# Normalizing retention on VectorE one tile at a time, one bank for four score products, and a buffer of its own for half of the last down-projection weights

## The chip, the cores and the metric

The kernel runs on one core of a Trainium2 chip. The engines are TensorE (PE: matmul, with its weight loads shown as PEld), VectorE (DVE), ScalarE (ACT), GpSimd (POOL) and SyncE (SP, which here only issues transfers). The metric is the time of one execution on the device in microseconds; lower is better. Before the change the median of three runs is 1147.84 us (1147.78 to 1148.55).

## The reference, cut to what matters

One layer of a diffusion backbone works on 640 tokens of 1024 channels: 128 context tokens and 512 latent tokens. After a modulated RMSNorm two token mixers run side by side, a bidirectional retention and a grouped-query attention; both are gated and summed, and a gated MLP of width 2816 with a three-tap convolution follows. All numbers are fp32.

Two places matter here. The first is retention, which runs in chunks of 128 tokens with 8 heads (64 channels of q and k, 128 of v), and its norm per head:

```
scores = einsum("bhnid,bhnjd->bhnij", qc, kc) * intra_decay
intra  = einsum("bhnij,bhnjv->bhniv", scores, vc)
cross  = einsum("bhnid,nbhdv->bhniv", qc * q_decay, s_prev)
o      = rms_scale(o_f + o_b)              # per token and head, over 128 channels
yr     = silu(rg) * o
```

The second is the end: `x = x + g2 * ((silu(g) * a) @ w_down)`, and one last RMSNorm over the 1024 channels of each token.

## The kernel before, in words

**Tiles.** The 640 tokens are five tiles of 128 tokens. Fp32 products are made from a high and a low part (fp32r), so that one product is three matmuls (`mm3`, lines 157 to 159; in transposed form lines 195 to 197, and 1579 to 1582 in the MLP). A weight block of 1024 or 2048 columns is loaded into one of two `weights.raw` buffers (line 134, issued by SP). ScalarE then copies its high part into a `weights.wh` tile, of which there are eight (line 145), and the low part is made either by VectorE (line 150) or by a negated ScalarE copy and an accumulating transfer that POOL issues (lines 147 and 148). In the MLP's units the same is done by lines 1556 to 1564.

**Retention.** Two groups of four heads times five tiles make ten steps. They pass through three functions in a pipeline. `ret_a` (lines 920 to 942) transposes q on TensorE into a PSUM bank (927), copies it out twice on ScalarE (932) and once with the decay on VectorE (936), transposes k into a second bank (939), and copies that on ScalarE (941). `ret_b`, one step later, makes the four score products of the heads (949) and multiplies them by the decay matrix on VectorE (952). `ret_c`, one step later still, makes the outputs (960 and 962), squares and copies them on ScalarE (965 and 966) and sums the squares on VectorE (967). Behind the last tile of each group, `ret_d` works out the inverse root of the five tiles (14 small VectorE instructions, lines 208 to 220) and scales the five tiles (973). PSUM tiles named `aux` have three banks: a step needs one for q, one for k, two for the scores and one for the output.

Beside the ten steps runs `rg0`, the gate projection for the first four heads, whose matmuls fill TensorE between the steps; one part of it is drawn behind every third yield of `retention`. Its evacuation (lines 1001 to 1004) takes tanh on ScalarE and then two VectorE instructions, the second of which multiplies the gate into the same `f0.s` tiles that line 973 scales. The projection for the other four heads follows.

**Order.** In this stage a planner sets the order on each engine ahead of time, from the order in the program and from costs of its own, and it also chooses which free PSUM bank a tile gets. On the chip every engine then works strictly through its own list. In the MLP the order of TensorE is written out by hand (`seq`), and those of the other engines are left to the planner.

**The end.** The MLP makes the 2816 channels in pairs of 128. `w_down` is applied in groups of four channel blocks; the last group (`last_group`, lines 1655 to 1670) is split in two column halves (g = 0 and 1), and each loads 2048 weight columns into one `weights.raw` buffer. Of these the first 1024 are prepared early (`prep(0)`) and used for tiles 0 to 3 while the last convolutions and gates (lines 1366 to 1382) are still being made; the second 1024 (`prep(1)`) follow. Then `last` runs: the rest of the matmuls, the gated residual add on VectorE (1454 and 1459), the squares on ScalarE (1476), and the final norm and the stores. The load for g = 1 comes in `pump`, which calls a group's `load` as soon as fewer than two loaded groups still have weights to prepare.

Of the kernel before, what the change touches and what calls it, by code (L numbers as in the profile page):

```python
# [18 lines left out]
P = 128  # L19
# [51 lines left out]
def hybrid_step(ctx: ExitStack, tc: tile.TileContext, a: dict, o: dict):  # L71
    nc = tc.nc
# [18 lines left out]
    V = nc.vector  # L91
# [11 lines left out]
    for i, n in enumerate(("c", "c_ctx", "norm1_g", "norm2_g")):  # L103
        src = a[n].rearrange("(k p) -> k p", p=P) if n == "c_ctx" else a[n].rearrange("o (k p) -> (o k) p", p=P)
# [24 lines left out]
    def load_w(src, kk, n, lo_eng=None):  # L129
        return w_split(w_raw(src, kk, n), kk, n, lo_eng)  # L130

    def w_raw(src, kk, n):
        raw = wp([P, 4 * 512], F32, tag="raw", bufs=2)
        nc.sync.dma_start(raw[:, :kk * n].rearrange("p (k n) -> p k n", n=n), src.rearrange("(k p) n -> p k n", p=P))
        return raw

    def w_split(raw, kk, n, lo_eng=None):
        hs, ls = [], []
        step = 1024 // n
        for k0 in range(0, kk, step):  # L140
            w = min(step, kk - k0) * n
            rv = raw[:, k0 * n:k0 * n + w]
            hi = wp([P, 1024], F32R, tag="wh", bufs=8)[:, :w]
            lo = wp([P, 1024], F32R, tag="wh", bufs=8)[:, :w]
            nc.scalar.copy(hi, rv)  # L145
            if lo_eng == "dma":
                nc.scalar.activation(lo, rv, AF.Copy, scale=-1.0)
                nc.gpsimd.dma_start(lo, rv, accum_op=ALU.add)
            else:
                (lo_eng or V).tensor_sub(lo, rv, hi.bitcast(F32))  # L150
            for k in range(w // n):
                hs.append(hi[:, k * n:(k + 1) * n])
                ls.append(lo[:, k * n:(k + 1) * n])
        return hs, ls
# [6 lines left out]
    def run(gen):  # L161
        for _ in gen:
            pass
# [39 lines left out]
    def rsqrt(pool, ss, n, inv_n, post=1.0):  # L203
        m = pool([P, n], tag=f"nm{n}", bufs=2)
        it = pool([P, n], I32, tag=f"ni{n}", bufs=2)
        y = pool([P, n], tag=f"ny{n}", bufs=2)
        tt = pool([P, n], tag=f"nt{n}", bufs=2)
        V.tensor_scalar(m, ss, inv_n, EPS, op0=ALU.mult, op1=ALU.add)
        V.tensor_scalar(it, m.bitcast(I32), 1, None, op0=ALU.logical_shift_right)
        V.tensor_scalar(y.bitcast(I32), it, -1, 0x5F3759DF, op0=ALU.mult, op1=ALU.add)  # L210
        V.tensor_scalar(m, m, -0.5, None, op0=ALU.mult)
        for _ in range(3):
            if n == 1:
                V.scalar_tensor_tensor(tt, y, m, y, op0=ALU.mult, op1=ALU.mult)
            else:
                V.tensor_mul(tt, y, y)
                V.tensor_mul(tt, tt, m)
            V.scalar_tensor_tensor(y, tt, 1.5, y, op0=ALU.add, op1=ALU.mult)  # L218
        if post != 1.0:
            V.tensor_scalar(y, y, post, None, op0=ALU.mult)  # L220
        return y
# [84 lines left out]
    aux = Pool("aux1", 3, space=PSUM)  # L306
# [273 lines left out]
    for i in (1, 0):  # L580
        ct, st = ctab[i], stab[i]
# [70 lines left out]
    aux = Pool("aux2", 2, space=PSUM)  # L652
# [132 lines left out]
    aux = Pool("aux3", 3, space=PSUM)  # L785
# [20 lines left out]
    for c in range(KD):  # L806
        if c % 2 == 0:
            w = load_w(a["w_att_o"][0, :, c * P:(c + 2) * P], 8, 256)
# [14 lines left out]
    def r2k():  # L823
        return rp([P, 512], tag="r2k", bufs=7)
# [3 lines left out]
    dmat = rp([P, 8, P])  # L828
# [87 lines left out]
    st = states()  # L916
# [26 lines left out]

    def ret_b(t, hh, qt, kt):
        at_ = r2k().rearrange("p (h i) -> p h i", h=4)
        psc = [aux([P, 512], tag="aux") for _ in range(2)]
        for j in range(2):
            for par in range(2):
                nc.tensor.matmul(psc[par][:, j * P:(j + 1) * P], kt[:, j * P:(j + 1) * P], qt[:, j, par, :],
                                 start=True, stop=True)  # L950
        for par in range(2):
            V.tensor_mul(at_[:, par::2, :], psc[par][:, :256].rearrange("p (h i) -> p h i", h=2),
                         dmat[:, 4 * hh + par:4 * hh + 4:2, :])
        return at_

    def ret_c(t, hh, qd, at_):
# [12 lines left out]
    def ret_d(hh):  # L969
        rso = rsqrt(rs2, sso[:, hh].rearrange("p t h -> p (t h)"), 4 * NT, 1.0 / P, post=0.5)  # L970
        for t in range(NT):
            ov = rvv[hh][:, :, t, :]
            nc.gpsimd.tensor_mul(ov, ov, rso[:, 4 * t:4 * t + 4].unsqueeze(2).to_broadcast([P, 4, P]))  # L973

    def conv_load(after):
        nc.gpsimd.tensor_copy(cw[:, :, 0], after)
        for i in range(3):
            nc.sync.dma_start(cw[:, i, :], a["conv_w"][0, i].rearrange("(c p) -> p c", p=P))
        nc.sync.dma_start(cw[:, 3, :], a["conv_b"][0].rearrange("(c p) -> p c", p=P))

    def retention():
        gr = [(t, hh) for hh in range(2) for t in range(NT)]
        sa, sb = {}, {}
        for i in range(len(gr) + 2):
            if i < len(gr):
                sa[i] = ret_a(*gr[i])
            if i == 1:
                conv_load(sa[0][2][:, :4])
            if 0 <= i - 1 < len(gr):
                sb[i - 1] = ret_b(*gr[i - 1], sa[i - 1][0], sa[i - 1][2])  # L990
            yield
            if 0 <= i - 2 < len(gr):
                ret_c(*gr[i - 2], sa[i - 2][1], sb[i - 2])
                if i - 2 in (4, 9):
                    ret_d(gr[i - 2][1])
            yield

    def evac_rg(g):
        def f(t, ps):
            th = r2k()  # L1000
            nc.scalar.activation(th, ps, AF.Tanh, scale=0.5)
            V.scalar_tensor_tensor(th, th, 1.0, ps, op0=ALU.add, op1=ALU.mult)
            ov = rvv[g][:, :, t, :]
            V.tensor_mul(ov, ov, th.rearrange("p (h d) -> p h d", h=4))
        return f
# [6 lines left out]
    for i, _ in enumerate(retention()):  # L1012
        if i % 3 == 2:
            next(rg0, None)
# [242 lines left out]
    w_up, w_down = a["w_up"][0], a["w_down"][0]  # L1257
# [21 lines left out]
    def h2_trans(t):  # L1279
        c = int(t == 0)  # L1280
        c0 = t * P
        for g in range(2):
# [6 lines left out]
            for j in range(4):  # L1289
# [5 lines left out]
                else:  # L1295
# [5 lines left out]
                   first=(lambda: [x + y for x, y in zip(*wo0[1:3])], lambda: wo0[3]))  # L1301
    run(wo_a)
    wo = [w_split(wo1[1], 4, 512), load_w(w_out[512:, 512:], 4, 512)]
    raw = w_raw(w_up[:, :256], 8, 256)
# [32 lines left out]
    t7 = Pool("t7", side="right")  # L1337
# [306 lines left out]
    fs = list(range(NF - 4, NF))  # L1644
# [10 lines left out]
    def last_group(g):  # L1655
        st = {}

        def load():
            st["raw"] = w_raw(w_down[fs[0] * P:, g * 512:(g + 1) * 512], 4, 512)

        def prep(h):
            def go():
                w = w_split(st["raw"][:, 1024 * h:1024 * (h + 1)], 2, 512, "dma" if h else None)
                ws[g] = [x + y for x, y in zip(ws.get(g, ([], [])), w)]
            return go

        items = [lambda t=t: last_mm(t, g * 512, 512, (0, 1)) for t in (0, 2, 1, 3)]
        return load, [(prep(0), 2, items)], items, prep(1)
# [118 lines left out]
```

## Time and profile before

| what | before |
|---|---|
| median of three runs | 1147.84 us |
| the profiled execution's own time | 1147.93 us |
| its span, first to last instruction | 1146.1 us |
| TensorE busy | 1116.3 us (97%) |
| weight loads of TensorE busy | 1006.6 us (88%) |
| VectorE busy | 841.5 us (73%) |
| ScalarE busy | 598.8 us (52%) |
| POOL busy | 154.4 us (13%) |
| granted clock of TensorE | 0.998 |

All times below are microseconds from the start of the span. The page gives busy time by engine, the waits say which instruction waited for which, and the timeline lists instructions in order of time with start, duration, engine, line, output and inputs, and, in square brackets, the idle time of the engine before it and what ended it. A TensorE row's duration reaches over the start of the next row, since matmuls are pipelined: the distance from one start to the next is what one matmul costs.

### The profile page before, as it was taken

The page shows a single profiled execution, that of the slowest core. Times are in us where ns is not written, and L with a number is a line of the kernel's source. Part 1 is how long each engine was busy: PE and PEld are TensorE (multiplying, and loading weights), DVE is VectorE, ACT ScalarE, POOL GpSimd, SP SyncE. Part 2 cuts the span into 40 slices and gives each one's busy share as a digit, 9 for nine tenths or more (in the row PEclk, how much of TensorE's full clock was granted, in tenths as well). Part 3 has the DMA queues.
Part 4 walks back from the last instruction along what each step waited for, and adds up shares of the span by engine and source line. Part 5 has one row for each costly group of instructions (what it writes and reads, how often), then busy time and mean ns, then how long its engine had stood idle before and what let it go on. Part 6 is the DMA issues. An engine that isn't in the chain of part 4 may idle for free.

```text
span 1146.1 us, 17450 instructions
## 1 busy us (share of the span) xinstructions
PE 1116.3 (97%) x6725; PEld 1006.6 (88%) x6725; DVE 841.5 (73%) x1464; ACT 598.8 (52%) x1127; POOL 154.4 (13%) x181
## 2 busy tenths in 40 slices
PE   5999999999999999999999999999999999999996
PEld 4788899999978878878999989999899899899985
DVE  4566977759969946565847648968687598589878
ACT  5355756553243334543346436678557476575463
POOL 0042200000000010021003132012111111121012
PEclk9999999999999999999999999999999999999999
DMA  9742111007846343311218937456657646666462
GB/s 308 242 150 74 38 37 38 26 13 230 305 141 218 130 138 48 39 38 37 74 37 174 286 134 220 128 117 121 142 142 159 155 76 165 136 122 167 119 129 110
DMA packets 132611, 147.92 MB, mean 129 GB/s; under 512 B 27160, under 2 KB 101992, under 8 KB 132272
## 3 DMA queue, kind: packets, MB, share of 16 engines
q1 hardware_dynamic: 103152, 115.59, 31.4%
q0 software_dynamic: 29104, 31.10, 17.2%
q8 instruction: 53, 0.87, 0.3%
q14 instruction: 30, 0.25, 0.1%
q10 hardware_dynamic: 272, 0.11, 0.0%
HBM read 115.05 MB, written 8.67 MB: 108 GB/s over the span
## 4 chain that ended last, share of the span: by engine, by line
PE 83%; DVE 8%; ACT 5%; issue 2%; DMA 1%; ACTq 0%; DVEq 0%; POOL 0%
DMA weights.raw.414_10656<-in_w_down 1%; DVE x1.u1.1_6299 L1459 1%; DMA weights.raw.247_7695<-in_w_down 0%; DMA const.u2.2_72<-in_b_mod 0%; DVE x1.u1.1_6299 L1508 0%; DVE x1.u1.1_6299 L1471 0%; DVE weights.raw.395_10305 L1556 0%; DVE x1.u1.1_6299 L1266 0%; DVE x1.u1.1_6299 L1466 0%; PE mm3.mm.72_6140 L1139 0%; DVE acts.u2.2_91 L430 0%; PE mm1.mm.11_294 L159 0%; PE mm7.mm.8_7506 L1582 0%; PE mm7.mm.41_9512 L1581 0%; PE mm7.mm.38_9263 L1582 0%
## 5 line engine op out<-in xcount | busy, mean ns | idle before, releaser
L814 POOL DMA_DIRECT2D spill.u2.2_2891<-f1.s.1_1160 x1 | 0.6, 594 | 129.7 <-DVE mod.u3.3_2846 L602 129.7
L1111 POOL DMA_DIRECT2D weights.wh.164_5834<-weights.raw.156_5767 x1 | 1.3, 1327 | 86.6 <-DVE f1.s.9_5178 L1150 86.6
L1596 DVE TENSOR_TENSOR t7.u4.4_6787<-t7.u4.4_6787,const.u1.1_70 128x320 f32<-128x320 f32 x10 | 4.9, 493 | 10.1 <-ACT const.u1.1_70 L1595 10.1
L910 DVE SCALAR_TENSOR_TENSOR ret2.u1.1_4174<-ret2.u1.1_4174,const.u11.11_86 64x128 f32<-64x128 f32 x24 | 6.8, 339 | 6.4 <-ACT ret2.u1.1_4174 L903 6.3
L973 POOL TENSOR_TENSOR f0.s.5_3419<-f0.s.5_3419,ret2.ny20.13_4765 128x512 f32<-128x512 f32 x5 | 5.5, 1124 | 38.4 <-DVE ret2.ny20.13_4765 L220 38.4
L912 DVE SCALAR_TENSOR_TENSOR ret2.u1.1_4174<-ret2.u1.1_4174,const.u11.11_86 64x128 f32<-64x128 f32 x24 | 6.6, 381 | 4.7 <-ACT ret2.u1.1_4174 L905 4.7
L150 DVE TENSOR_TENSOR weights.wh.113_4364<-weights.raw.111_4361,weights.wh.112_4363 128x1024 fp32r<-128x1024 f32 x1 | 1.2, 1224 | 11.4 <-ACT weights.wh.112_4363 L145 11.4
L427 ACT CAST acts.u1.1_90<-f0.s.2_104 128x640 fp32r<-128x640 f32 x4 | 2.9, 728 | 9.5 <-DVE f0.s.2_104 L425 9.5
L973 POOL TENSOR_TENSOR f0.s.6_3420<-f0.s.6_3420,ret2.ny20.20_4981 128x512 f32<-128x512 f32 x5 | 5.0, 1040 | 19.7 <-DVE ret2.ny20.20_4981 L220 19.7
L297 POOL DMA_DIRECT2D mod.acc.24_3626<-in_b_mod x2 | 1.7, 861 | 43.5 <-ACT weights.wh.94_3862 L145 43.5
L582 POOL TENSOR_TENSOR p1.u1.1_604<-p1.u3.3_608,p1q.u1.1_598 128x512 f32<-128x512 f32 x1 | 1.3, 1313 | 44.3 <-DMA p1.u4.4_610<-in_cache_k 44.3
L551 ACT ACTIVATE f0.s.3_710<-f0.s.3_710,p1q.ny20.11_878 128x128 f32<-128x128 f32 x20 | 6.0, 388 | 2.5 <-DVE p1q.ny20.11_878 L218 2.5
L444 PE MATMUL aux1.aux.1_134<-const.u1.1_70,const.u2.2_72 80*128 80x80 f32 x1 | 0.4, 367 | 6.9 <-DMA const.u2.2_72<-in_b_mod 6.9
L427 ACT CAST acts.u1.1_90<-f0.s.1_103 128x640 fp32r<-128x640 f32 x4 | 2.9, 726 | 8.0 <-DVE f0.s.1_103 L425 7.9
L145 ACT CAST weights.wh.67_3284<-weights.raw.66_3282 128x1024 fp32r<-128x1024 f32 x1 | 1.1, 1050 | 11.3 <-PE mm3.mm.8_3125 L196 11.3
L145 ACT CAST weights.wh.77_3516<-weights.raw.76_3514 128x1024 fp32r<-128x1024 f32 x1 | 1.1, 1055 | 11.2 <-PE mm3.mm.16_3382 L196 11.2
L1113 DVE TENSOR_TENSOR weights.wh.152_5686<-weights.raw.151_5632,weights.wh.152_5686 128x512 fp32r<-128x512 f32 x1 | 0.7, 697 | 8.3 <-ACT weights.wh.152_5686 L1104 8.3
L1470 DVE TENSOR_TENSOR x1.u1.1_6299<-x1.u1.1_6299,gate.u1.1_6285 128x512 f32<-128x512 f32 x10 | 6.7, 684 | 0.0
L1503 POOL TENSOR_TENSOR x1.u1.1_6299<-x1.u1.1_6299,weights.raw.422_10856 128x512 f32<-128x512 f32 x3 | 4.9, 1632 | 12.6 <-ACT x1.tm.111_10869 L1476 9.8
L145 ACT CAST weights.wh.92_3858<-weights.raw.91_3856 128x1024 fp32r<-128x1024 f32 x1 | 1.1, 1057 | 10.5 <-PE mm3.mm.26_3653 L158 10.5
L551 ACT ACTIVATE p1.u4.4_610<-p1.u4.4_610,p1.ny10.15_660 128x128 f32<-128x128 f32 x10 | 3.0, 388 | 6.5 <-DVE p1.ny10.15_660 L218 6.5
L150 DVE TENSOR_TENSOR weights.wh.83_3657<-weights.raw.81_3654,weights.wh.82_3656 128x1024 fp32r<-128x1024 f32 x1 | 1.2, 1224 | 7.0 <-ACT weights.wh.82_3656 L145 7.0
(6899 smaller groups left out, 4935.1 us busy)
## 6 DMA issues: line engine op xcount, KB each, us to landing
spill.u1.1_2890<-x1.u1.1_6299 POOLq DMA_DIRECT2D x5, 512.0 KB, 3.6
xin.u1.1_102<-in_x_sample SPq DMA_DIRECT2D x4, 512.0 KB, 4.7
p0.u5.5_119<-in_w_mod SPq DMA_DIRECT2D x2, 1024.0 KB, 9.9
p0.u6.6_125<-in_w_mod SPq DMA_DIRECT2D x2, 1024.0 KB, 14.6
p0.u7.7_128<-in_w_mod SPq DMA_DIRECT2D x2, 1024.0 KB, 12.8
gate.u1.1_6285<-spill.u3.3_2892 SPq DMA_DIRECT2D x2, 1024.0 KB, 4.2
x1.u1.1_6299<-in_x_sample SPq DMA_DIRECT2D x4, 512.0 KB, 10.4
out_y_sample<-x1.u1.1_6299 SPq DMA_DIRECT2D x8, 256.0 KB, 2.0
```

The source lines that it names most:

```text
L145: nc.scalar.copy(hi, rv)
L150: (lo_eng or V).tensor_sub(lo, rv, hi.bitcast(F32))
L297: nc.gpsimd.dma_start(accs[v][0:1, c, :], a["b_mod"][0:1, col:col + DM], accum_op=ALU.add)
L427: nc.scalar.copy(hT[0][:, k, :], xk)
L551: nc.scalar.activation(x[:, j], x[:, j], AF.Copy, scale=rstd[:, j:j + 1])
L910: V.scalar_tensor_tensor(Ss[0:64, hh, st + 1, j], Ss[0:64, hh, st, j], cdsel[0:64, h:h + 1], Ss[0:64, hh, st + 1, j], op0=ALU.mult, op1=AL ...
L912: V.scalar_tensor_tensor(Ss[64:128, hh, 2 - st, j], Ss[64:128, hh, 3 - st, j], cdsel[64:128, h:h + 1], Ss[64:128, hh, 2 - st, j], op0=ALU. ...
L973: nc.gpsimd.tensor_mul(ov, ov, rso[:, 4 * t:4 * t + 4].unsqueeze(2).to_broadcast([P, 4, P]))
L1459: V.tensor_add(x1[:, t, gs], x1[:, t, gs], down_mul(ps, t, c0))
L1470: V.tensor_mul(x1[:, t, gs], x1[:, t, gs], gb[:, t == 0, gs])
L1503: eng.tensor_mul(x, x, fg[:, c0:c0 + 512])
L1596: V.tensor_sub(his[1], his[1], u3[i])
```

## The change

There are three parts. In `ret_b` the four score products go to the four quarters of one PSUM bank, where they went to two halves of two banks, and one VectorE instruction of 512 columns multiplies them by the decay, where two of 256 did. In `ret_d` the scaling goes from GpSimd to VectorE, and one tile is scaled per step of the following pipeline instead of five together; for the second group the five follow at the end of `retention`. In `last_group` the first half of the weights for g = 1 gets a buffer of its own (`rawl`, in pool `t7`) and a transfer of its own; the second half goes to a `weights.raw` buffer, by another transfer.

```diff
 def ret_b(t, hh, qt, kt):
-        psc = [aux([P, 512], tag="aux") for _ in range(2)]
+        psc = aux([P, 512], tag="aux")
         for j in range(2):
             for par in range(2):
-                nc.tensor.matmul(psc[par][:, j * P:(j + 1) * P], kt[:, j * P:(j + 1) * P], qt[:, j, par, :],
+                h = 2 * j + par
+                nc.tensor.matmul(psc[:, h * P:(h + 1) * P], kt[:, j * P:(j + 1) * P], qt[:, j, par, :],
                                  start=True, stop=True)
-        for par in range(2):
-            V.tensor_mul(at_[:, par::2, :], psc[par][:, :256].rearrange("p (h i) -> p h i", h=2),
-                         dmat[:, 4 * hh + par:4 * hh + 4:2, :])
+        V.tensor_mul(at_, psc.rearrange("p (h i) -> p h i", h=4), dmat[:, 4 * hh:4 * hh + 4, :])
...
 def ret_d(hh):
         for t in range(NT):
+            yield
             ov = rvv[hh][:, :, t, :]
-            nc.gpsimd.tensor_mul(ov, ov, rso[:, 4 * t:4 * t + 4].unsqueeze(2).to_broadcast([P, 4, P]))
+            V.tensor_mul(ov, ov, rso[:, 4 * t:4 * t + 4].unsqueeze(2).to_broadcast([P, 4, P]))
...
 def retention():
+        norm = iter(())
         for i in range(len(gr) + 2):
...
             yield
+            next(norm, None)
             if 0 <= i - 2 < len(gr):
                 ret_c(*gr[i - 2], sa[i - 2][1], sb[i - 2])
                 if i - 2 in (4, 9):
-                    ret_d(gr[i - 2][1])
+                    norm = ret_d(gr[i - 2][1])
+                    next(norm)
             yield
+        run(norm)
...
 def last_group(g):
         def load():
-            st["raw"] = w_raw(w_down[fs[0] * P:, g * 512:(g + 1) * 512], 4, 512)
+            src = w_down[fs[0] * P:, g * 512:(g + 1) * 512]
+            if g == 0:
+                raw = w_raw(src, 4, 512)
+                st["raw"] = [raw[:, 1024 * h:1024 * (h + 1)] for h in range(2)]
+                return
+            first = t7([P, 1024], tag="rawl")
+            nc.sync.dma_start(first.rearrange("p (k n) -> p k n", n=512), src[:2 * P].rearrange("(k p) n -> p k n", p=P))
+            st["raw"] = [first, w_raw(src[2 * P:], 2, 512)]

         def prep(h):
             def go():
-                w = w_split(st["raw"][:, 1024 * h:1024 * (h + 1)], 2, 512, "dma" if h else None)
+                w = w_split(st["raw"][h], 2, 512, "dma" if h else None)
```

## Prediction

> **What bounds the kernel.** I read the page first, then busy time in stretches, then TensorE's waits, and the timelines where these point.
>
> ```profile
> span 1146.1 us, 17450 instructions
> PE 1116.3 (97%) x6725; PEld 1006.6 (88%) x6725; DVE 841.5 (73%) x1464; ACT 598.8 (52%) x1127; POOL 154.4 (13%) x181
> ```
>
> TensorE is the bound nearly everywhere, so an edit is worth the time in which TensorE stands, plus what it moves in the tail behind the last matmul. Stretches around the two edited places (columns: stretch, then PE, PEld, DVE, ACT, POOL busy):
>
> ```profile
> 490.00:500.00 10.00, 7.76 (x48) 6.22 (x47) 7.26 (x8) 5.35 (x11) 4.82 (x5) 1.00 0.05 13
> 500.00:510.00 10.00, 9.90 (x79) 8.79 (x78) 6.15 (x11) 4.47 (x10) 0.00 (x0) 1.00 0.27 94
> 1100.00:1110.00 10.00, 9.40 (x57) 8.47 (x56) 4.33 (x9) 3.58 (x5) 0.01 (x1) 1.00 0.36 107
> 1110.00:1120.00 10.00, 9.01 (x40) 6.93 (x38) 7.28 (x10) 6.30 (x9) 1.72 (x2) 1.00 0.74 157
> 1120.00:1130.00 10.00, 9.86 (x42) 7.71 (x43) 9.16 (x13) 3.62 (x10) 3.49 (x3) 1.00 0.01 2
> ```
>
> TensorE's waits, the longest here:
>
> ```profile
> PE aux3.aux.57_4861 L960 <- DVE ret.r2k.67_4845 L936: 2.2, 1, 2.2
> ```
>
> **Part 1, scaling on VectorE.** The 2.2 us hole, on VectorE, POOL and TensorE:
>
> ```profile
> 490.48 0.39 PE L157 MATMUL mm3.mm.41_4360<-weights.wh.119_4640,acts.u1.1_90 128*128 128x512 f32 x1
> 490.71 0.39 PE L158 MATMUL mm3.mm.41_4360<-weights.wh.120_4641,acts.u1.1_90 128*128 128x512 f32 x1
> ...
> 492.41 1.51 DVE L1004 TENSOR_TENSOR f0.s.5_3419<-f0.s.5_3419,ret.r2k.64_4823 128x512 f32<-128x512 f32 x1 [1.58 <-POOL f0.s.5_3419 L973]
> 493.85 2.06 DVE L150 TENSOR_TENSOR weights.wh.128_5080<-weights.raw.126_5077,weights.wh.127_5079 128x1024 fp32r<-128x1024 f32 x1
> 495.82 0.68 DVE L936 TENSOR_TENSOR ret.r2k.67_4845<-aux3.aux.53_4836,ret.u3.3_3418 128x512 f32<-128x512 f32 x1
> 497.09 1.21 DVE L150 TENSOR_TENSOR weights.wh.130_5084<-weights.raw.126_5077,weights.wh.129_5083 128x1024 fp32r<-128x1024 f32 x1
> 501.05 0.69 DVE L1004 TENSOR_TENSOR f0.s.5_3419<-f0.s.5_3419,ret.r2k.70_4886 128x512 f32<-128x512 f32 x1
> 489.34 5.48 POOL L973 TENSOR_TENSOR f0.s.5_3419<-f0.s.5_3419,ret2.ny20.13_4765 128x512 f32<-128x512 f32 x5 [38.44 <-DVE ret2.ny20.13_4765 L220]
> 493.92 0.40 PE L158 MATMUL mm3.mm.42_5002<-weights.wh.123_5010,acts.u1.1_90 128*128 128x512 f32 x1
> 496.56 0.49 PE L960 MATMUL aux3.aux.57_4861<-f0.s.6_3420,ret.r2k.63_4802 128*128 128x128 f32 x2 [2.24 <-DVE ret.r2k.67_4845 L936]
> ```
>
> The gate product (L1004) waits 1.58 us for POOL's scaling of its tile; then it and the weight subtraction (L150) run beside POOL at 1.51 and 2.06 us, where without POOL the same shapes take 0.69 and 1.21. Behind them stands the q product (L936), which frees the bank that the output matmul (L960) needs. The delay is 1.58 + 0.82 + 0.85 = 3.25 us on VectorE; on TensorE, 496.56 − 493.92 less one 512-column step (490.48 to 490.71, 0.23) is 2.4 us.
>
> The change takes POOL out: producer and consumer stand on one engine in program order, nothing runs beside them, and the 2.4 us go. In exchange VectorE gets ten 128x512 products at 0.69 (the L1004 row has the same shape and operands' places). The first five: 3.45 us into five steps. VectorE is busy 7.26 + 6.15 = 13.4 of the 20 us there, of which 1.67 is the slowing; with them it is about 15.2, and it waits for ScalarE's square before its sum (L967), which is the gap that hides them:
>
> ```profile
> 505.89 0.69 DVE L967 TENSOR_REDUCE const.u13.13_88<-ret.r2k.74_4924 128x4 f32<-128x512 f32 x1 [2.05 <-ACT ret.r2k.74_4924 L965]
> 514.17 0.18 DVE L220 TENSOR_SCALAR ret2.ny20.20_4981<-ret2.ny20.20_4981 128x20 f32<-128x20 f32 x1
> 519.75 1.23 DVE L150 TENSOR_TENSOR weights.wh.133_5189<-weights.raw.131_5186,weights.wh.132_5188 128x1024 fp32r<-128x1024 f32 x1 [5.40 <-ACT weights.wh.132_5188 L145]
> ```
>
> The other five follow at 514.35 and end at 517.8, inside the 5.40 us in which VectorE is idle. Without that cover each costs 0.69, 6.9 in all. Term: **−2.4**.
>
> **Part 2, one bank for the scores.** One step (TensorE, then ScalarE's copy of k and VectorE's product with q):
>
> ```profile
> 486.36 0.38 PE L939 MATMUL aux3.aux.49_4797<-const.u1.1_70,ret.u5.5_3422 128*128 128x128 f32 x2
> 486.58 0.61 PE L949 MATMUL aux3.aux.50_4803<-ret2.u2.2_4175,ret2.rkT.10_4739 128*128 128x128 f32 x4
> 486.95 0.48 PE L159 MATMUL mm3.mm.40_4359<-weights.wh.119_4640,acts.u2.2_91 128*128 128x512 f32 x1
> 487.26 0.40 PE L157 MATMUL mm3.mm.41_4360<-weights.wh.117_4636,acts.u1.1_90 128*128 128x512 f32 x1
> 487.76 0.71 PE L949 MATMUL aux3.aux.51_4804<-ret2.u2.2_4175,ret2.rkT.10_4739 128*128 128x128 f32 x4
> 487.33 0.37 ACT L941 COPY ret2.rkT.15_4800<-aux3.aux.49_4797 128x256 f32<-128x256 f32 x1
> 487.58 0.68 DVE L936 TENSOR_TENSOR ret.r2k.62_4795<-aux3.aux.48_4786,ret.u3.3_3418 128x512 f32<-128x512 f32 x1
> ```
>
> Three banks hold q, k and the first scores, so the second score bank is k's, free when L941 ends at 487.70, and TensorE starts at 487.76. From 487.26 to there is 0.50, where a 512-column step takes 0.23: 0.27 lost, and the four score passes then take 0.56 to the next start instead of the first bank's 0.37, of which some 0.1 is refilling. That is about 0.3 in each of ten steps, 3.0 us, which busy time hardly shows, since the rows overlap. With one bank the eight passes run on end, to about 487.5, and the step's fourth bank is the output's, which is asked for later, behind fill. The wait goes (−3.0) or moves to the output (0, if the planner puts no fill ahead of it). Since the planner judged k's copy 0.3 too early, I take half: **−1.5**. VectorE's two products of 0.42 become one of 0.68 like L936, a small gain that lies in its idle time.
>
> The Trainium skill, "Perfetto Trace Analysis", section "Identifying the Most-Contended Engine", holds that matmul busy time is a poor measure of TensorE's headroom and weight-load busy a better one; PEld at 88% beside PE at 97% agrees. By it part 2 would be nearer −3.0, and the sum below 1140.0.
>
> **Part 3, a buffer for half the last weights.** SP, ScalarE, TensorE and VectorE at the end:
>
> ```profile
> 1100.03 0.38 SPq L134 DMA_DIRECT2D weights.raw.414_10656<-in_w_down  x1
> 1106.42 1.05 ACT L145 CAST weights.wh.416_10707<-weights.raw.414_10656 128x1024 fp32r<-128x1024 f32 x1 [6.55 <-DMA weights.raw.414_10656<-in_w_down]
> 1111.35 0.42 ACT L1599 COPY t7.u2.2_6785<-mm7.mm.59_10637 128x320 f32<-128x320 f32 x1
> 1106.84 0.40 PE L159 MATMUL acc7.acc.52_10765<-weights.wh.412_10652,gt.gt1.26_10512 128*128 128x512 f32 x1
> 1107.84 0.42 PE L1579 MATMUL mm7.mm.59_10637<-acts.u1.1_90,weights.wh.415_10673 128*128 128x320 f32 x1 [0.60 <-ACT const.u1.1_70 L1595]
> 1109.72 0.39 PE L157 MATMUL mm7.mm.62_10789<-weights.wh.412_10652,gt.gt0.25_10511 128*128 128x512 f32 x1
> 1118.54 0.45 PE L159 MATMUL acc7.acc.51_10758<-weights.wh.418_10846,gt.gt1.28_10797 128*128 128x512 f32 x1
> 1119.97 0.50 PE L157 MATMUL acc7.acc.51_10758<-weights.wh.418_10846,gt.gt0.27_10796 128*128 128x512 f32 x1 [0.99 <-ACT gt.gt0.27_10796 L1381]
> 1121.17 0.39 PE L157 MATMUL acc7.acc.53_10817<-weights.wh.420_10851,gt.gt0.27_10796 128*128 128x512 f32 x1
> 1121.37 0.69 DVE L1454 TENSOR_TENSOR x1.tm.110_10866<-acc7.acc.51_10758,gate.u1.1_6285 128x512 f32<-128x512 f32 x1 [0.59 <-PE acc7.acc.51_10758 L159]
> 1141.47 1.41 DVE L1508 SCALAR_TENSOR_TENSOR x1.u1.1_6299<-x1.u1.1_6299,t7.ry.33_10985,weights.raw.422_10856 128x512 f32<-128x512 f32 x2
> ```
>
> The last load goes out when its buffer comes free at 1100.03, and ScalarE, in line, stands 6.55 us at the first copy from it. Queued behind that copy are the evacuation L1595, the copies of the second weight halves, L1599 and the last convolutions and gates. TensorE waits for them twice: 1107.84 − 1106.84 − 0.23 = 0.77, and the four steps from 1118.54 to 1121.17 take 2.63 instead of 0.92, 1.71 lost; together 2.5. TensorE itself needs the late weights (wh.416) only behind 1109.72.
>
> With a buffer of its own the first half is there before ScalarE comes to it, so L1595 runs when its product ends. Is the next wait as long? The product that L1599 copies ends near 1109.72 and was copied at 1111.35, because weight copies stood ahead. Now it ends at 1108.95, and L1599 can go 2.4 us earlier; the last gate's high part, 2.4 earlier than 1119.97, is there at 1117.6, and TensorE asks for it at 1118.54 + 0.23 − 0.77 = 1118.0. So that wait goes too, by 0.4 us. The second half of the weights still goes out at 1100.03, with half the bytes, and its copies are not needed before 1118. Behind TensorE, VectorE works nearly without a pause (9.16 of 10 in 1120 to 1130) from 1121.37 to 1142.88 and sets the end, so the end moves with L1454: **−2.5**.
>
> When does the new transfer run? It waits for no weight buffer, and the planner draws such loads far forward:
>
> ```profile
> 696.99 0.34 SPq L1469 DMA_DIRECT2D x1.tm.93_10163<-spill.u1.1_2890  x1
> ```
>
> This load (tile number 10163) belongs to work near 1060 (raw.414 above, 1100 us, has 10656) and ran at 697. So rawl's 512 KB go out around 650 to 700 at the cost of at most a part of the 6.4 us (1106.42 − 1100.03) that 1024 KB took, 3.2 as an upper bound, if a transfer of that time were needed at once; no wait of TensorE there ends on a transfer, so I take 0. If instead it is issued right behind the load before it, it has some 6 us until 1100; 0 too.
>
> **Sum.** Against the profiled execution's own 1147.93 (span 1146.1 and 1.8 around it; median of the runs 1147.84): −2.4 − 1.5 − 2.5 = −6.4, **1141.5**. TensorE's shift near 500 reaches the end only if nothing after it is held by something else; loads, copies and evacuations in between are released by buffers that TensorE or its followers free, so they shift with it.
>
> **Rivals.**
> (a) *The tail gives nothing*: the planner puts the second-half copies or other work ahead of the gates, and they end when they did. For it: it did put weight copies ahead of L1599. Against: the 6.55 us of standing leave room for all of them. 1147.93 − 3.9 = 1144.0.
> (b) *Retention gives nothing*: the planner makes a new order there, and another in-order wait of 2 to 4 us takes the hole's place, as it did with L150 ahead of L936. Against: POOL is gone from the path. 1147.93 − 2.5 = 1145.4.
> (c) *No part does what it says*: TensorE's waits only change names. 1147.9. Against it stand 6.55 us and 3.25 us with a named cause each.
> (d) *Slower, VectorE on the path*: the output takes q's bank instead of k's, and L936, which frees it, stands behind a scaling. L936 ends at 488.26, 488.95 with 0.69 ahead of it; TensorE, done with the scores at 487.5, would stand 1.4 us in five steps and 0.8 in the other five, 11 us. With −2.4, −3.0 and −2.5 that is 1151.0; it decides from 0.8 us per step. For it: the planner picks the bank, from costs that missed k's copy by 0.3. Against: k's bank is free 0.6 earlier than q's. The Trainium skill speaks on its side ("Perfetto Trace Analysis", section "Optimizing Scalar/DVE Operations": work may go from a saturated VectorE to GpSimd, the reverse of this change); VectorE's 13.4 of 20 us here is not saturation.
>
> **Chances.** Forecast 60%, own range 1139.5 to 1143.2 (part 2 at both ends, and 0.4 for small waits that come and go in the planner's orders); (a) 13%, (b) 9%, (c) 7%, (d) 11%. The range runs from 1139.5 to 1145.8: forecast, (a) and (b). A change under 0.2% (2.3 us) can't be told from none here. Faster: the forecast, (a) and half of (b), 78%; same: (c) and the other half, 11%; slower: (d), 11%.
>
> **What would show it.** Part 1: no POOL row of L973's shape, L150 at 1.2 throughout, no TensorE wait on L936. Part 2: one L949 group of eight passes per step, none ending a wait on L941; the output's first matmul without a wait. Part 3: rawl's issue long before 1090, ScalarE's 6.55 us gone, no TensorE wait on L1595 or L1381, and L1454 about 2.5 nearer to the end of the last product. The forecast is wrong if TensorE waits at L960 for L936 or L941 in each step, or if the chain still passes through a transfer at the end.

## The result and the profile after

The changed kernel takes 1141.36 us, median of four runs (1141.22 to 1141.63); the kernel before, 1148.19 on the same chip (1147.78 to 1148.55). The ratio is 0.9941, interval 0.9924 to 0.9958: faster by 6.8 us (4.8 to 8.7 by the interval). The profiled execution took 1141.31 us of its own time, against 1147.93 before.

The page of the changed kernel, span and busy time of each engine:

```profile
span 1139.5 us, 17424 instructions
PE 1113.7 (98%) x6725; PEld 1007.3 (88%) x6725; DVE 845.4 (74%) x1464; ACT 599.6 (53%) x1127; POOL 143.1 (13%) x171
```

VectorE works 3.9 us longer than before (841.5), POOL 11.3 shorter (154.4), and TensorE 2.6 shorter although it has the same 6725 instructions. So 4.0 of the 6.6 us were time in which TensorE was not counted as busy, and 2.6 lay inside its busy rows. The same five stretches as before (columns: PE, PEld, DVE, ACT, POOL busy):

```profile
490.00:500.00 10.00, 10.00 (x74) 8.96 (x73) 7.16 (x12) 6.23 (x12) 0.00 (x0) 1.00 0.00 0
500.00:510.00 10.00, 10.00 (x58) 8.70 (x57) 9.52 (x25) 2.56 (x5) 0.00 (x0) 1.00 0.35 107
1100.00:1110.00 10.00, 10.00 (x51) 8.49 (x50) 6.35 (x8) 5.77 (x9) 1.71 (x2) 1.00 0.61 143
1110.00:1120.00 10.00, 10.00 (x45) 8.10 (x44) 7.53 (x11) 3.46 (x8) 1.66 (x1) 1.00 0.08 14
1120.00:1130.00 10.00, 10.00 (x56) 8.49 (x54) 9.69 (x20) 5.88 (x15) 4.67 (x4) 1.00 0.08 29
```

TensorE is full in all five; before, it was busy 7.76, 9.90, 9.40, 9.01 and 9.86.

**Retention, scaling.** VectorE's scalings (L973) and its neighbours after the change:

```profile
486.97 0.68 DVE L1008 TENSOR_TENSOR f0.s.5_3419<-f0.s.5_3419,ret.r2k.64_4804 128x512 f32<-128x512 f32 x1
487.57 1.28 DVE L973 TENSOR_TENSOR f0.s.5_3419<-f0.s.5_3419,ret2.ny20.13_4753 128x512 f32<-128x512 f32 x2
488.81 0.69 DVE L936 TENSOR_TENSOR ret.r2k.67_4827<-aux3.aux.46_4818,ret.u3.3_3418 128x512 f32<-128x512 f32 x1
...
496.21 1.22 DVE L150 TENSOR_TENSOR weights.wh.128_5060<-weights.raw.126_5057,weights.wh.127_5059 128x1024 fp32r<-128x1024 f32 x1
...
507.08 3.10 DVE L973 TENSOR_TENSOR f0.s.6_3420<-f0.s.6_3420,ret2.ny20.20_4961 128x512 f32<-128x512 f32 x5
515.78 1.23 DVE L150 TENSOR_TENSOR weights.wh.133_5169<-weights.raw.131_5166,weights.wh.132_5168 128x1024 fp32r<-128x1024 f32 x1 [5.60 <-ACT weights.wh.132_5168 L145]
```

The gate product (L1008 is L1004 of before) no longer waits and takes 0.68 instead of 1.51; the weight subtraction takes 1.22 instead of 2.06. The second group's five scalings run in one go and lie ahead of a wait of 5.60 us, as forecast.

**Retention, scores.** One step on TensorE, and ScalarE's copy of k:

```profile
482.77 0.49 PE L927 MATMUL aux3.aux.42_4769<-const.u1.1_70,ret.r2k.61_4770 128*128 128x128 f32 x3
483.10 0.38 PE L939 MATMUL aux3.aux.43_4780<-const.u1.1_70,ret.u5.5_3422 128*128 128x128 f32 x2
483.32 1.06 PE L950 MATMUL aux3.aux.44_4786<-ret2.u2.2_4175,ret2.rkT.10_4729 128*128 128x128 f32 x8
484.50 1.16 PE L959 MATMUL aux3.aux.45_4809<-f0.s.6_3420,ret.r2k.59_4731 128*128 128x128 f32 x8
...
484.07 0.37 ACT L941 COPY ret2.rkT.15_4783<-aux3.aux.43_4780 128x256 f32<-128x256 f32 x1
```

The eight score passes are one group now. Eight passes at 0.111 (the median distance between such starts) end at 483.32 + 0.89 = 484.21; the output starts at 484.50, right after ScalarE's copy of k ends at 484.44. So a wait of up to 0.29 has moved from the second half of the scores to the output. The planner gave the output k's bank and put no fill ahead of it in this step. That the output takes k's bank shows in TensorE's waits, where it ends a wait for the copy of k (L941); one of the two listed in this stage:

```profile
PE aux3.aux.25_4546 L959 <- ACT ret2.rkT.6_4537 L941: 0.2, 1, 0.2
```

**The end.** SP, ScalarE and VectorE:

```profile
656.72 0.58 SPq L1669 DMA_DIRECT2D t7.rawl.25_10636<-in_w_down  x1
...
1094.17 0.43 ACT L1603 COPY t7.u1.1_6764<-mm7.mm.56_10499 128x320 f32<-128x320 f32 x1
1094.48 1.05 ACT L145 CAST weights.wh.416_10689<-t7.rawl.25_10636 128x1024 fp32r<-128x1024 f32 x1
...
1114.78 0.69 DVE L1458 TENSOR_TENSOR x1.tm.110_10848<-acc7.acc.51_10740,gate.u1.1_6265 128x512 f32<-128x512 f32 x1 [0.82 <-PE acc7.acc.51_10740 L159]
...
1134.89 1.41 DVE L1512 SCALAR_TENSOR_TENSOR x1.u1.1_6279<-x1.u1.1_6279,t7.ry.34_10967,weights.raw.422_10838 128x512 f32<-128x512 f32 x2
```

The new transfer is issued at 656.72, 438 us ahead of its first use, and ScalarE's copy from it starts at 1094.48 without standing (before: 6.55 us). VectorE's first residual product comes 6.59 us earlier (1121.37 to 1114.78) and its last instruction 6.58 earlier (1141.47 to 1134.89): the whole gain has been made before the last products, and nothing is given back behind them.

**Where the time came from.** TensorE's lost time can be summed without the busy shares, which hide stalls shorter than the overlap of two rows: for each two matmuls in a row, the distance of their starts less the median distance of the same two shapes in the same trace. All kernels of this study, by that sum (us) and by the median of their runs. The runs were made in several groups, each beside the kernel before, whose median there stands in the third column; medians of different groups are to be compared by way of it:

| kernel | median of runs | before, same group | lost, 440 to 520 | lost, 1100 to 1140 |
|---|---|---|---|---|
| before | 1148.19 | 1148.19 | 9.09 | 3.08 |
| changed | 1141.36 | 1148.19 | 4.98 | 0.49 |
| part 1 alone | 1145.18 | 1147.60 | 6.65 | 3.12 |
| part 2 alone | 1143.13 | 1147.60 | 5.23 | 2.73 |
| part 3 alone | 1145.48 | 1147.60 | 9.09 | 0.48 |
| parts 2 and 3 | 1141.32 | 1147.87 | 4.96 | 0.48 |
| changed, POOL scales one tile per step | 1141.64 | 1147.60 | 4.99 | 0.49 |
| changed, VectorE scales five together | 1141.63 | 1147.35 | 4.83 | 0.49 |
| changed, scores first | 1139.35 | 1147.35 | 3.38 | 0.46 |
| scores first, two score banks | 1139.83 | 1147.87 | 3.75 | 0.48 |
| scores first, POOL scales | 1140.33 | 1147.87 | 3.89 | 0.45 |

From before to changed it is 4.11 in retention and 2.59 at the end, 6.70 together; the profiled execution became 6.62 shorter. Not all of the sum in retention is waits: some 2.0 of it before and 1.35 after lie between the fill's own matmuls, in pieces of about 0.09 that end no listed wait, and their number changes from kernel to kernel (21 before, 13 after). Their cause is not known. Counting only the distances that end at a score or an output product, the stage loses 6.24 before, 3.80 with part 1 alone, 2.96 with part 2 alone, 2.81 changed and 1.23 with the scores first.

### The profile page after: what moved, and what is told of

Its sections match the earlier page's. It is cut to its first block, busy times and chain, and to the rows that moved or that the text cites. A ratio compares the mean times of both kernels' runs of the same rounds, so it can differ in the third digit from the quotient of the medians.

```text
span 1139.5 us, 17424 instructions
## 1 busy us (share of the span) xinstructions
PE 1113.7 (98%) x6725; PEld 1007.3 (88%) x6725; DVE 845.4 (74%) x1464; ACT 599.6 (53%) x1127; POOL 143.1 (13%) x171
## 4 chain that ended last, share of the span: by engine, by line
PE 89%; DVE 5%; ACT 4%; issue 2%; DMA 1%; ACTq 0%; DVEq 0%; POOL 0%
DVE x1.u1.1_6279 L1463 1%; DMA weights.raw.247_7675<-in_w_down 0%; DMA const.u2.2_72<-in_b_mod 0%; DVE x1.u1.1_6279 L1512 0%; DVE x1.u1.1_6279 L1270 0%; PE mm3.mm.72_6120 L1143 0%; DVE acts.u2.2_91 L430 0%; PE mm1.mm.11_294 L159 0%; PE mm7.mm.8_7486 L1586 0%; PE mm7.mm.59_10617 L1586 0%; PE mm7.mm.44_9725 L1585 0%; PE mm7.mm.32_8989 L1585 0%; PE mm7.mm.29_8756 L1586 0%; PE mm7.mm.26_8507 L1586 0%; PE mm3.mm.69_5986 L1146 0%
## 5 line engine op out<-in xcount | busy, mean ns | idle before, releaser
L1600 DVE TENSOR_TENSOR t7.u4.4_6767<-t7.u4.4_6767,const.u1.1_70 128x320 f32<-128x320 f32 x10 | 4.9, 494 | 11.3 <-ACT const.u1.1_70 L1599 11.3
L145 ACT CAST weights.wh.67_3284<-weights.raw.66_3282 128x1024 fp32r<-128x1024 f32 x1 | 1.1, 1051 | 11.3 <-PE mm3.mm.8_3125 L196 11.3
L1600 DVE TENSOR_TENSOR t7.u3.3_6766<-t7.u3.3_6766,const.u1.1_70 128x320 f32<-128x320 f32 x9 | 4.4, 489 | 2.5 <-ACT const.u1.1_70 L1599 2.5
```

The costliest lines, as they stand in the source:

```text
L1600: V.tensor_sub(his[1], his[1], u3[i])
```

## The experiments

All nine do the whole computation. Each was timed five times, parts 1 and 3 alone eleven times, beside the kernel before (third column of the table). The differences below are to its median in the same group.

**1. Each part alone.** The theory on trial is the prediction's sum: the parts add up. Its rival: the second bank of the scores is also what makes VectorE's delay reach TensorE, so part 2 takes the hole too.

Part 1 alone:

```diff
+            yield
             ov = rvv[hh][:, :, t, :]
-            nc.gpsimd.tensor_mul(ov, ov, rso[:, 4 * t:4 * t + 4].unsqueeze(2).to_broadcast([P, 4, P]))
+            V.tensor_mul(ov, ov, rso[:, 4 * t:4 * t + 4].unsqueeze(2).to_broadcast([P, 4, P]))
...
+                    norm = ret_d(gr[i - 2][1])
+                    next(norm)
...
```

> Part 1 alone: the scaling on VectorE, one tile per step; two score banks and the old last load stay. Theory of the prediction (three causes that add up): the 2.4 us hole at the output matmul is gone, the standing at the second score bank (0.3 in each step) and the tail stay: 2.4 us less than before, some 1145.7. Rival (the bank is what matters: the output needs q's bank, and VectorE with five more products frees it late): the hole is only smaller, under 1 us gained.

Measured: 1145.18 (1144.29 to 1146.08), ratio 0.9981 [0.9972, 0.9990], 2.4 less than before. That is what the prediction's theory gave, and the rival (under 1 us) falls. The hole is gone, and the 0.3 per step of the two score banks is still there: 486.27 + 0.23 leaves 0.27 to 486.77, with these TensorE rows:

```profile
485.37 0.38 PE L939 MATMUL aux3.aux.49_4792<-const.u1.1_70,ret.u5.5_3422 128*128 128x128 f32 x2
485.59 0.61 PE L949 MATMUL aux3.aux.50_4798<-ret2.u2.2_4175,ret2.rkT.10_4739 128*128 128x128 f32 x4
485.96 0.47 PE L159 MATMUL mm3.mm.40_4359<-weights.wh.119_4640,acts.u2.2_91 128*128 128x512 f32 x1
486.27 0.40 PE L157 MATMUL mm3.mm.41_4360<-weights.wh.117_4636,acts.u1.1_90 128*128 128x512 f32 x1
486.77 0.71 PE L949 MATMUL aux3.aux.51_4799<-ret2.u2.2_4175,ret2.rkT.10_4739 128*128 128x128 f32 x4
```

Part 2 alone:

```diff
-        psc = [aux([P, 512], tag="aux") for _ in range(2)]
+        psc = aux([P, 512], tag="aux")
...
+        V.tensor_mul(at_, psc.rearrange("p (h i) -> p h i", h=4), dmat[:, 4 * hh:4 * hh + 4, :])
```

> Part 2 alone: one bank for the four score products; the scaling stays on GpSimd, all five tiles at once. Theory of the prediction (three causes that add up): 1.5 us less than before, some 1146.6, with the hole of 2.4 us still there. Rival (the bank is the cause of the hole too): the output takes k's bank, so a late product with q no longer stops it; the hole goes although VectorE still waits 1.6 us for GpSimd, and the run is 3.9 us faster than before, 1144.2; part 1 would then add nothing.

Measured: 1143.13, ratio 0.9965 [0.9952, 0.9977], 4.5 less than before (2.6 to 5.5 by the interval), not 1.5. The rival's mechanism is the one that came out. By TensorE's lost time it is 3.86 in retention (3.28 of it at the scores and outputs; the rival gave 3.9), and 0.35 at the end, where one of two waits got shorter for a reason that was not looked into. VectorE still waits for POOL here, and for longer than before. TensorE, VectorE and POOL of part 2 alone:

```profile
487.29 0.38 PE L939 MATMUL aux3.aux.47_4833<-const.u1.1_70,ret.u5.5_3422 128*128 128x128 f32 x2
487.50 1.06 PE L950 MATMUL aux3.aux.48_4839<-ret2.u3.3_4176,ret2.rkT.15_4788 128*128 128x128 f32 x8
488.68 0.49 PE L959 MATMUL aux3.aux.49_4845<-f0.s.6_3420,ret.r2k.63_4790 128*128 128x128 f32 x2
...
489.14 1.51 DVE L1003 TENSOR_TENSOR f0.s.5_3419<-f0.s.5_3419,ret.r2k.64_4809 128x512 f32<-128x512 f32 x1 [2.63 <-POOL f0.s.5_3419 L972]
490.58 0.68 DVE L936 TENSOR_TENSOR ret.r2k.67_4831<-aux3.aux.46_4822,ret.u3.3_3418 128x512 f32<-128x512 f32 x1
...
486.07 5.48 POOL L972 TENSOR_TENSOR f0.s.5_3419<-f0.s.5_3419,ret2.ny20.13_4753 128x512 f32<-128x512 f32 x5 [36.16 <-DVE ret2.ny20.13_4753 L220]
```

VectorE stands 2.63 us and is slowed to 1.51, and the q product (L936), which frees q's bank aux.46, starts only at 490.58. Yet the output (L959) started at 488.68, 1.9 us ahead of it: it cannot have q's bank. With two score banks the second takes k's, and q's is what is left for the output; with one, the output takes k's. In this order VectorE also has no weight subtraction between the gate product and the q product, where the kernel before had one of 2.06 us; why the planner left it out there was not tried, and the 1.9 us do not depend on it.

Part 3 alone:

```diff
-            st["raw"] = w_raw(w_down[fs[0] * P:, g * 512:(g + 1) * 512], 4, 512)
...
+            first = t7([P, 1024], tag="rawl")
...
+            st["raw"] = [first, w_raw(src[2 * P:], 2, 512)]
...
```

> Part 3 alone: half of the last weights in a buffer of its own. Theory: TensorE's 0.77 and 1.71 us in the last 45 us are gone and the tail behind it moves with it: 2.5 us less than before, some 1145.6. Rival (in the changed kernel the tail was better because retention was, through the planner's order): under 1 us.

Measured: 1145.48, ratio 0.9981 [0.9972, 0.9990], 2.1 less than before: the theory holds, and the rival (under 1 us) falls. TensorE has no wait in the last part that the profile lists, and its lost time there falls by 2.60 (3.08 to 0.48); the hole of retention is still there. In the trace of part 3 alone:

```profile
PE aux3.aux.57_4861 L960 <- DVE ret.r2k.67_4845 L936: 2.2, 1, 2.2
```

The three parts alone gain 2.4 + 4.5 + 2.1 = 9.0, together 6.8. The medians are uncertain by about a microsecond each, but the lost time in retention says the same: 2.44 for part 1 and 3.86 for part 2, together 4.11. The 2.2 between them is the size of the hole: parts 1 and 2 both remove it.

**2. Parts 2 and 3, with the scaling left on POOL.** If that is so, part 1 adds nothing to the other two. The diff, as in experiments 3 and 4, is against the changed kernel.

```diff
-            yield
             ov = rvv[hh][:, :, t, :]
-            V.tensor_mul(ov, ov, rso[:, 4 * t:4 * t + 4].unsqueeze(2).to_broadcast([P, 4, P]))
+            nc.gpsimd.tensor_mul(ov, ov, rso[:, 4 * t:4 * t + 4].unsqueeze(2).to_broadcast([P, 4, P]))
...
-                    norm = ret_d(gr[i - 2][1])
-                    next(norm)
+                    ret_d(gr[i - 2][1])
...
```

> The changed kernel without its first part: the five scalings stay on GpSimd in one go, the scores share a bank, the last load has its buffer. Bank theory (what carries VectorE's delay to TensorE is that the output takes the bank that q's product frees; with one score bank it takes another, so it does not matter which engine scales): 1141.2 to 1141.8, within 0.5 us of the changed kernel, and VectorE still shows a wait of 1.5 us or more on POOL's scaling near 490 with no TensorE wait of over 0.5 us beside it. Additive theory (the prediction's sum, where part 1 is worth 2.4 by itself): 1143.7 or more.

Measured: 1141.32 (1140.81 to 1142.72), ratio 0.9946 [0.9933, 0.9960]. That is the changed kernel's time (0.9941). The bank theory holds, the additive one falls. Here too VectorE waits for POOL and TensorE does not:

```profile
489.16 1.51 DVE L1003 TENSOR_TENSOR f0.s.5_3419<-f0.s.5_3419,ret.r2k.64_4809 128x512 f32<-128x512 f32 x1 [2.63 <-POOL f0.s.5_3419 L972]
490.59 0.68 DVE L936 TENSOR_TENSOR ret.r2k.67_4831<-aux3.aux.46_4822,ret.u3.3_3418 128x512 f32<-128x512 f32 x1
491.19 0.67 DVE L952 TENSOR_TENSOR ret.r2k.68_4838<-aux3.aux.48_4839,ret.u2.2_3417 128x512 f32<-128x512 f32 x1
...
488.69 0.49 PE L959 MATMUL aux3.aux.49_4845<-f0.s.6_3420,ret.r2k.63_4790 128*128 128x128 f32 x2
```

**3. Which half of part 1: the engine or the spreading?** Both with parts 2 and 3. First the spreading with POOL as the engine:

```diff
-            V.tensor_mul(ov, ov, rso[:, 4 * t:4 * t + 4].unsqueeze(2).to_broadcast([P, 4, P]))
+            nc.gpsimd.tensor_mul(ov, ov, rso[:, 4 * t:4 * t + 4].unsqueeze(2).to_broadcast([P, 4, P]))
```

> The changed kernel with the scaling back on GpSimd, but one tile per step as in the change. Theory (the engine is the cause): GpSimd takes 1.03 us per tile, slows VectorE's products beside it by 0.8 each, and the gate product waits for it; up to 2.4 us more than the changed kernel, 1142.5 to 1143.8. Rival (spreading out and one bank are enough): within 0.5 us of the changed kernel's 1141.4.

Measured: 1141.64, ratio 0.9949 [0.9937, 0.9962]: the changed kernel's time. The theory that the engine matters, mine then, fell. Then VectorE without the spreading:

```diff
-            yield
...
-                    norm = ret_d(gr[i - 2][1])
-                    next(norm)
+                    ret_d(gr[i - 2][1])
...
```

> The changed kernel with the five scalings of the first group on VectorE in one go behind the inverse root, as they stood on GpSimd, instead of one per step. Theory of the prediction (VectorE's waits for ScalarE hide the scalings only if they are spread): 3.1 to 3.45 us of VectorE in one piece ahead of the next step's products with q and the scores; TensorE stands 0.5 to 2 us: 1141.9 to 1143.4. Rival (with one bank nothing of TensorE waits on VectorE soon enough): within 0.3 us of the changed kernel.

Measured: 1141.63, ratio 0.9947 [0.9935, 0.9959]. The rival holds: spreading them is not needed either. Five scalings in a row take 3.09 us and put the q product off to 491.05, and again TensorE doesn't wait for it: the output starts at 489.71. VectorE and TensorE of this kernel:

```profile
487.45 3.09 DVE L972 TENSOR_TENSOR f0.s.5_3419<-f0.s.5_3419,ret2.ny20.13_4753 128x512 f32<-128x512 f32 x5
490.45 0.69 DVE L1003 TENSOR_TENSOR f0.s.5_3419<-f0.s.5_3419,ret.r2k.64_4809 128x512 f32<-128x512 f32 x1
491.05 0.69 DVE L936 TENSOR_TENSOR ret.r2k.67_4831<-aux3.aux.46_4822,ret.u3.3_3418 128x512 f32<-128x512 f32 x1
...
489.71 0.49 PE L959 MATMUL aux3.aux.49_4845<-f0.s.6_3420,ret.r2k.63_4790 128*128 128x128 f32 x2
```

**4. The wait that moved to the output.** If the output waits only because it is asked for right behind k's transpose and the scores, another order of the program should remove it: the scores of step i−1 ahead of the transposes of step i.

```diff
 for i in range(len(gr) + 2):
+            if 0 <= i - 1 < len(gr):
+                sb[i - 1] = ret_b(*gr[i - 1], sa[i - 1][0], sa[i - 1][2])
             if i < len(gr):
                 sa[i] = ret_a(*gr[i])
             if i == 1:
                 conv_load(sa[0][2][:, :4])
-            if 0 <= i - 1 < len(gr):
-                sb[i - 1] = ret_b(*gr[i - 1], sa[i - 1][0], sa[i - 1][2])
```

> The changed kernel with the score products of a step ahead of the transposes of the next one, so that between a bank's filling and its next use lie six transposes or eight output passes. In the changed kernel the output starts about 0.2 to 0.3 us late in each step, behind ScalarE's copy of k. Theory (half of what part 2 could give was left there, as the prediction's middle value has it): 1 to 2 us less than the changed kernel, 1139.4 to 1140.4. Rival (the wait only moves, to the score product on VectorE or to the copies of q): within 0.5 us of it, or slower.

Measured: 1139.35 (1139.12 to 1140.02), ratio 0.9929 [0.9916, 0.9943]; 2.3 below the kernel with five scalings together, timed on the same chip (1141.15 to 1142.06). The theory holds, with the time at the lower bound of its range. TensorE and VectorE of this kernel:

```profile
483.79 1.06 PE L950 MATMUL aux3.aux.46_4819<-ret2.u3.3_4176,ret2.rkT.15_4790 128*128 128x128 f32 x8
484.60 0.48 PE L157 MATMUL mm3.mm.40_4359<-weights.wh.117_4628,acts.u1.1_90 128*128 128x512 f32 x1
...
486.54 0.60 PE L927 MATMUL aux3.aux.47_4825<-const.u1.1_70,ret.r2k.67_4826 128*128 128x128 f32 x4
486.98 0.38 PE L939 MATMUL aux3.aux.48_4836<-const.u1.1_70,ret.u5.5_3422 128*128 128x128 f32 x2
487.19 0.39 PE L959 MATMUL aux3.aux.49_4842<-f0.s.6_3420,ret.r2k.61_4769 128*128 128x128 f32 x2
...
486.18 0.69 DVE L952 TENSOR_TENSOR ret.r2k.66_4818<-aux3.aux.46_4819,ret.u2.2_3417 128x512 f32<-128x512 f32 x1
```

The output starts 0.21 after k's transpose with nothing lost between. Of the three banks q's and k's have only just been filled, so it has that of the scores (aux.46), which VectorE has read by 486.87, 0.32 before, while fill lay behind the scores. This version is faster than the kernel before by 8.0 us. The changed kernel was not timed on this chip, and the intervals of the two ratios overlap (0.9916 to 0.9943 and 0.9924 to 0.9958); that the order gains on it rests on the kernel with five scalings together, which takes the changed kernel's time, and on TensorE's lost time, 3.38 against 4.98.

**5. Is it the order or the number of banks?** The version with scores first, but with the two score banks of `ret_b` before the change:

```diff
-        psc = aux([P, 512], tag="aux")
+        psc = [aux([P, 512], tag="aux") for _ in range(2)]
...
```

> Scores first in the order, but with two score banks as before the change, and the scaling on VectorE and the load's buffer as in the changed kernel. Order theory (the 0.3 us per step come from asking for a bank right behind k's transpose, so calling the scores ahead of the transposes cures them whatever the number of banks): 1139.0 to 1140.0. Bank theory (five banks asked for per step out of three leave one wait per step in any order): 1141.5 to 1143.5, about what parts 1 and 3 alone give (1147.7 - 2.4 - 2.1 = 1143.2), with a TensorE wait on ScalarE's or VectorE's copy of about 0.3 us in most steps.

Measured: 1139.83 (1139.63 to 1141.03), ratio 0.9932 [0.9920, 0.9945], 1.5 below parts 2 and 3 on the same chip. The order theory holds: with the scores first, part 2 isn't needed either. TensorE's waits in this stage:

```profile
PE aux3.aux.19_4484 L949 <- ACT ret2.rkT.4_4481 L941: 0.3, 1, 0.3
PE aux3.aux.23_4526 L949 <- issue: 0.2, 1, 0.2
```

Both stand in the first two steps, and the first is for the copy of k that this score product itself reads; from the third step on no group of score or output products starts over 0.1 late. And the version with scores first and one bank, but with POOL scaling five tiles in one go, as in experiment 2:

```diff
-            V.tensor_mul(ov, ov, rso[:, 4 * t:4 * t + 4].unsqueeze(2).to_broadcast([P, 4, P]))
+            nc.gpsimd.tensor_mul(ov, ov, rso[:, 4 * t:4 * t + 4].unsqueeze(2).to_broadcast([P, 4, P]))
...
```

> Scores first, one score bank, the load's buffer, and the five scalings in one go on GpSimd. If the scaling's engine does not matter in this order either: within 0.5 us of the version with scores first and the scaling on VectorE (1139.0 to 1140.0). If with scores first the output again waits for a bank that stands behind VectorE's delay: 1141 to 1142, with a TensorE wait of 1 us or more near 490.

Measured: 1140.33 (1139.17 to 1140.60), ratio 0.9933 [0.9921, 0.9945]. The median falls between the two expectations. In the trace VectorE waits 1.72 us for POOL, and TensorE's longest wait near 490 is 0.3, where the second expected 1 or more:

```profile
PE aux3.aux.53_4897 L959 <- DVE ret.r2k.71_4874 L952: 0.3, 1, 0.3
...
488.96 1.52 DVE L1003 TENSOR_TENSOR f0.s.5_3419<-f0.s.5_3419,ret.r2k.64_4809 128x512 f32<-128x512 f32 x1 [1.72 <-POOL f0.s.5_3419 L972]
```

That 0.3 does come from the delay: the score product for which the output waits (L952) stands on VectorE behind the slowed gate product, with no pause between. So with the scores first the output hangs on a bank behind VectorE again, as the second expectation had it, but only with 0.3 us; whether this shows in the median stays open. Of the three versions with scores first none can be told from the others: their intervals overlap nearly wholly. The scores first with two banks and POOL's scaling together, that is the order and the load's buffer without parts 1 and 2, was not tried.

## Why the prediction was right, and where its split was wrong

Forecast 1141.5, measured 1141.36; the sum of −6.4 stands against −6.8 by the medians and −6.62 by the profiled executions. The runs themselves can't tell it that closely (4.8 to 8.7). By its own steps:

- **Part 1, −2.4.** What it said of VectorE came true in each row: no POOL row of the scaling, 1.58 us of waiting gone, 1.51 and 2.06 down to 0.68 and 1.22, the ten scalings hidden. Alone it is worth 2.4 by the medians and 2.44 by TensorE's lost time in retention. In the change it is worth nothing that can be measured (1141.32 without it). The step that failed is "the change takes POOL out … and the 2.4 us go": the hole had two conditions, a late q product and an output that needs q's bank, and the prediction counted the removal of the first while its own part 2 removed the second. It had both rows: L960 waited for L936, and the second score bank was k's.
- **Part 2, −1.5 between 0 and −3.0.** With the hole already gone (part 1 alone to changed, in retention) it is 6.65 − 4.98 = 1.67. The middle was taken because the wait could go or move to the output. It moved in part: before, the second half of the scores started 0.12 to 0.33 late in nine of the ten steps, in the changed kernel the output 0.22 to 0.43 late in six. That the middle came so near is in part luck: that the planner was 0.3 out gives no half, and of the 1.67 only 0.99 lies at the scores and outputs (3.80 to 2.81); 0.64 are the small pieces between fill matmuls, which the prediction did not count. The sum below 1140.0, with −3.0 for this part, did not come about. And 1.67 is its worth behind part 1; taken first, it is 3.86 (3.28 at the scores and outputs), which the range of this term did not hold, since the hole was booked elsewhere.
- **Part 3, −2.5.** 2.60 by TensorE's lost time at the end, 2.1 by the medians. ScalarE's 6.55 us are gone, both TensorE waits with them, and the early transfer (656.72, forecast 650 to 700) cost nothing that shows. What it would have cost if issued late was not tried.
- **Sum.** It came out because each term was worked out from another stall of TensorE in the kernel before: the hole, the standing at the second score bank in a step without the hole, and the waits at the end. A hole can be taken away only once, and it was counted once. Its owner was wrong, and the size of part 2 was in part luck.
- **Rivals.** (a) fell by the lost time at the end (3.08 to 0.49), (b) by that in retention (9.09 to 4.98), (c) with them. (d), the output in q's bank behind a scaling, did not come about: even with five scalings together, where L936 starts at 491.05 behind 3.09 us of them, TensorE loses nothing more (4.83 against 4.98), because the output takes k's bank, as the argument against (d) had it. The same argument, "k's bank is free 0.6 earlier than q's", would have told that part 2 alone closes the hole.
- **The list of what would show it.** All of it held but for two points. The output's first matmul does wait for L941, in five of the ten steps, and starts 0.28 to 0.43 late there; such a wait in each step was the sign of a wrong forecast. And the first residual product came no nearer to the last matmul: from start to start it is 15.03 before (1121.37 to 1136.40) and 15.02 after (1114.78 to 1129.80), since both of TensorE's waits lay ahead of both.

The Trainium skill, "Perfetto Trace Analysis", section "Optimization Strategy", says that the same gap repeating on the engine that should be saturated can mean that there isn't enough PSUM for the next tile. The 0.27 per step was such a gap, and giving each step one bank less (part 2) did shorten it, which agrees. But with the scores first and two score banks it is gone as well (the waits in experiment 5): the banks were enough, and the order in which they were asked for was not good.

## What to carry to other kernels

Behind a stall, look for the chain of buffers as well as for the slow producer: a late instruction costs only what waits for its result or for the bank that it frees, and an edit that changes who gets which bank can make the producer's delay free of charge. When two edits touch the same stall, each alone shows its full worth and the second adds nothing, so work out each term on what the others leave. When summing small gaps, look at which rows hold them, since some of the sum may have nothing to do with the edit. A gap of 0.3 us per step that busy shares hide is found by the distance between starts, and may be cured by asking for the buffers in another order, at no cost in memory.

## What the runs showed of the hardware

In these runs the slowing of VectorE beside POOL goes with where its operands lie. In the rows of parts 2 and 3 above, L1003 (both inputs in SBUF) takes 1.51 us beside POOL instead of 0.69, while L936 right behind it, with one input in a PSUM bank, takes its usual 0.68 although POOL works on until 491.57:

```profile
486.09 5.48 POOL L972 TENSOR_TENSOR f0.s.5_3419<-f0.s.5_3419,ret2.ny20.13_4753 128x512 f32<-128x512 f32 x5 [36.16 <-DVE ret2.ny20.13_4753 L220]
```

And POOL can be the one that pays. In the kernel where POOL scales one tile per step, VectorE's subtraction had begun 0.11 us ahead of it:

```profile
494.56 2.01 POOL L973 TENSOR_TENSOR f0.s.5_3419<-f0.s.5_3419,ret2.ny20.13_4753 128x512 f32<-128x512 f32 x1 [4.38 <-DVE f0.s.5_3419 L1008]
...
494.45 1.22 DVE L150 TENSOR_TENSOR weights.wh.128_5060<-weights.raw.126_5057,weights.wh.127_5059 128x1024 fp32r<-128x1024 f32 x1
```

VectorE takes its usual 1.22, and POOL's scaling 2.01 instead of the 1.04 that the other single one takes in the same kernel (at 503.18). The Trainium skill, "SBUF — State Buffer", section "Who interferes with whom", says both: a VectorE instruction with two SBUF inputs contends with a GpSimd instruction that reads SBUF, one with at most one doesn't, outside the two-port modes, and issue order decides who waits. These rows agree with it.
